# Emitting a triangular inverse one step at a time, with some of its VectorE instructions held in program order, and asking for one transfer of a recurrent chain before another

## The chip, the cores and the metric

The kernel runs on one core of one Trainium2 chip. A core has a matrix engine (TensorE, PE in the profile, with its weight loads as PEld), a vector engine (VectorE, DVE), a scalar engine (ScalarE, ACT), a general engine (GpSimd, POOL) and a sync engine (SyncE, SP). Each takes its own instructions in a fixed order and waits on semaphores for the others. Here SP issues the loads of weights, and POOL the transfers to and from scratch memory in HBM. The metric is the device time of one execution in microseconds (us), lower is better; the kernel before has a median of 1120.82 us in 3 runs (1118.6 to 1121.67).

## The reference, cut to what matters

One layer of a hybrid encoder over 512 tokens of 1024 channels. A normalised input is projected by one wide matrix; from the projections come a gated short convolution, a gated linear recurrence, and an RWKV-7 recurrence, which are merged by gates and projected; a squared-ReLU MLP and a last norm follow.

```python
h = rms_norm(x, norm1_g)
pa, pb, pg, pc = split(h @ w_in)                      # conv, linear recurrence, gates, RWKV-7
y_a = b_a * causal_dwconv(c_a * x_a)                  # "ab" in the kernel, with y_b
y_b = rg_lru(causal_dwconv(x_b)) * gelu(g_b)
def step(state, inp):                                 # RWKV-7, 16 heads of 64, over 512 tokens
    sa = einsum('bhvk,bhk->bhv', state, -kk_t)
    state = state * w_t + sa[..., None] * (kk_t * a_t) + v_t[..., None] * k_t
    y_t = einsum('bhvk,bhk->bhv', state, r_t)         # r is the receptance
m = gate_a * y_a + gate_b * y_b + gate_c * y_c
x = x + m @ w_out
x = rms_norm(x + square(relu(rms_norm(x) @ w1)) @ w2)
```

## The kernel before, in words

All large matrix products are done in three passes on split numbers: a weight tile `raw` (128x1024) is loaded by SP, ScalarE casts it to a rounded high part `whi` (L147, `ac.copy` in `split_w`), VectorE subtracts that from `raw` to give the low part `wlo` (the subtraction in `split_w`, shown as L104 because all `tensor_tensor` operations go through the helper `tt` there), and TensorE multiplies high by high (L168), high by low input (L169) and low by high (L170), 24 matmuls of 128x512 for a projection. There are two buffers of `raw` and three each of `whi` and `wlo`, so weights are ready at most about three projections ahead.

The RWKV-7 recurrence is done by chunks of 64 tokens. The 16 heads are four groups. For group g, `krv` computes keys, receptances and values (its row norm goes through a matmul `pn`, L433 and L434, on the halves `bh` and `bl` of squared keys, and back through VectorE: `rqw`, L194); `amat` computes the 64x64 matrices of each chunk; `inverse` inverts the triangular ones for 32 chunks and heads at once. In `inverse`, two transposes (L551) bring two 32x32 diagonal blocks each onto partitions; 31 steps of forward substitution follow on VectorE, each a multiplication into `dg` and an addition into `Z` (shapes 64x31 to 64x16x16 and down to 64x31), each of which depends on the one before; then three transposes (L568 twice, L571) bring the result back; then 32 small matmuls `pG` (L578) and 32 small `pT` (L588) make the off-diagonal block, and a POOL transfer stores the result in `ttd` (L591). I call the four calls inverse 0 to inverse 3.

The work of other parts is put between by `weave(crit, fill, r, base)`: it takes a step of the critical generator, adds `r` to a counter, and takes one step of the filler for each whole unit. A step of the critical generator is emitted under a raised priority (`base`, or the number that the generator yielded); the recorder then orders the instructions of each engine by priority and readiness by its own estimate of costs, so that the order in which they stand in the built program is fixed before it runs. The filler for inverse 0 to 2 is `fill_group`: 22 steps of the gate and recurrence branches `ab`, then `krv` of the next group with more of `ab` between, then 4 more; for inverse 3 it is `ab` alone. `keep_in_program_order` holds an instruction at its place in the program among those of its engine; before the change it is used for TensorE's small matmuls (by `pin`).

After the inverses, `chain` runs the 8 chunks one after another, with the rest of `ab` and then `gate` as filler. For each chunk `load_chunk` issues five transfers on POOL's queue, one chunk ahead: `sv` (values), `ax`, `tc` (the inverse), `bk` (keys) and, from chunk 1, `rt` (receptances). `bk` is used by the matmul `pS` (L664), `rt` by the matmul `py` (L645). After the chain come the output projection and the MLP, which the change does not touch.

Of the kernel before, what the change touches and what calls it, by code (L numbers as in the profile page):

```python
# [18 lines left out]
P = 128  # L19

OFF, OFFS, OFFP = 160, 20, 30
CP, CPI, CPK, CPC, CPN = 150, 0, 0, 20, 5
HOT = 6000

NINV, NG_T, N_LOAD = 19, 4, 6


N_KRV = 22
F_INV, F_KRV, F_GAP = 22, 16, 4
W3 = 3  # L30
R0, R1, R2, R3, R4 = 0.85, 1.15, 1.1, 1.7, 1.0
NWARM = 2
POOL_KT = (1, 3, 5, 6, 7)
S = 512
# [4 lines left out]
NG = 4  # L39
# [59 lines left out]
def block_kernel(ctx, tc, xt, win, par, mulr, sw, wout, w1, w2, fg, cst, eyes, out):  # L99
    nc = tc.nc  # L100
    v, ac, gp, pe, sy = nc.vector, nc.scalar, nc.gpsimd, nc.tensor, nc.sync

    def tt(o, a, b, op):
        return v.tensor_tensor(out=o, in0=a, in1=b, op=op)  # L104
# [7 lines left out]
    MUL, ADD, SUB, MAX = ALU.mult, ALU.add, ALU.subtract, ALU.max  # L112
# [431 lines left out]
    def inverse(g, G_):  # L544
        AXt = G_.AX
        Z = p1.tile([P, 2, 32, 32], F32, tag="Z", name="Z")
        la, xt = Z[64:128, 0], Z[64:128, 1]
        dg = p1.tile([P, 32, 32], F32, tag="dg", name="dg")
        tmp = dg[64:128].rearrange("p a b -> p (a b)")
        for b in range(2):  # L550
            v.transpose(la[32 * b:32 * b + 32].rearrange("l s t -> l t s"),  # L551
                        AXt[32 * b:32 * b + 32, 0, :, :, 32 * b:32 * b + 32].rearrange("s c e t -> s t (c e)"))
        gp.dma_start(xt.rearrange("l s t -> l (s t)"), eyes)

        yield
        yield
        for s in range(31):
            n, c = 31 - s, s + 1
            tv = tmp[:, 0:n * c].rearrange("l (c t) -> l c t", c=c)
            tt(tv, la[:, s, s + 1:32].unsqueeze(1).to_broadcast([64, c, n]),  # L560
               xt[:, 0:c, s:s + 1].to_broadcast([64, c, n]), MUL)
            tt(xt[:, 0:c, s + 1:32], xt[:, 0:c, s + 1:32], tv, ADD)
            if s % 2 == 1:
                yield
        TT = Z[0:64].rearrange("p a b c -> p (a b c)").rearrange("p (l t) -> p l t", t=L)
        gp.memset(TT[32:64, :, 0:32], 0.0)
        for b in range(2):
            v.transpose(TT[32 * b:32 * b + 32, :, 32 * b:32 * b + 32].rearrange("s l t -> s t l"),  # L568
                        xt[32 * b:32 * b + 32].rearrange("l s t -> l t s"))
        d1 = gs = dg  # L570
        v.transpose(d1[0:32], TT[0:32, :, 0:32])  # L571
        for _ in range(NINV):
            yield CPI
        for half in range(2):
            pg = pm.tile([P, 16, 32], F32, tag="pm", name="pG")
            for i in range(16):
                l = 16 * half + i
                pin(i, lambda: pe.matmul(pg[32:64, i], AXt[0:32, 0, l // 4, l % 4, 32:64], d1[0:32, l],  # L578
                                             start=True, stop=True))
            ac.copy(gs[32:64, 16 * half:16 * half + 16], pg[32:64])  # L580
            yield
        for _ in range(NG_T):
            yield 0
        for half in range(2):
            pg = pm.tile([P, 16, 32], F32, tag="pm", name="pT")
            for i in range(16):
                l = 16 * half + i
                pin(i + half, lambda: pe.matmul(pg[0:32, i], gs[32:64, l], TT[32:64, l, 32:64], start=True, stop=True))  # L588
            ac.copy(TT[0:32, 16 * half:16 * half + 16, 32:64], pg[0:32])
            yield  # L590
        gp.dma_start(ttd[:, :, g].rearrange("c t e x -> t c (e x)"),  # L591
                     TT.rearrange("t (c e) x -> t c (e x)", c=NC))
# [6 lines left out]
    def load_chunk(c):  # L599
        ax = C["ph2"].tile([P, NG, 2, 4, L], F32, tag="ax", name="ax", bufs=2)  # L600
        sv = C["ph2"].tile([P, NG, 4, L], F32, tag="sv", name="sv", bufs=2)
        tc_ = C["ph2"].tile([L, NG, 4, L], F32, tag="tc", name="tc", bufs=2)
        rt = C["ph2"].tile([P, 8, L], F32, tag="rt", name="rt", bufs=2)
        bk = C["ph2"].tile([P, 8, P], F32, tag="bk", name="bk", bufs=2)
        flat = lambda t: t.rearrange("p g a e t -> p (g a e t)") if len(t.shape) == 5 else \
            t.rearrange("p g e t -> p (g e t)") if len(t.shape) == 4 else t.rearrange("p x t -> p (x t)")
        gp.dma_start(flat(sv[64:128]), flat(vtd[c]))
        gp.dma_start(flat(ax), flat(axd[c]))
        gp.dma_start(flat(tc_), flat(ttd[c]))
        if c < NC - 1:  # L610
            gp.dma_start(flat(bk), flat(bkd[c]))
        if c > 0:
            gp.dma_start(flat(rt), flat(rtd[c]))
        return ax, sv, tc_, rt, bk

    def by_tile(t):
# [234 lines left out]
    for g in range(NG):  # L851
        if g:
            fgr = fill_group(g)
            weave(inverse(g - 1, GS[g - 1]), fgr, R1)
            drain(fgr)
        weave(amat(g, GS[g]), fl, 1.0)
    weave(inverse(NG - 1, GS[NG - 1]), fl, R2)
    pk_ctx.close()
    p1_ctx.close()
    ph2_ctx = ExitStack()  # L860
# [261 lines left out]
```

## Time and profile before

| what | value |
|---|---|
| median of 3 runs | 1120.82 us (1118.6 to 1121.67) |
| the profiled execution, its own time | 1119.94 us |
| its span in the trace | 1118.2 us |
| TensorE busy, matmuls | 1055.3 us, 94% of the span |
| VectorE busy | 746.4 us, 67% |
| ScalarE busy | 473.4 us, 42% |
| mean granted TensorE clock | 0.974 of full |

The 1.7 us between the profiled execution's time and its span lie around the span. The page shows the span in 40 slices of 28 us; the digits are busy tenths. Idle time of TensorE is named in the view of waits by what ended it; "us in total, times, longest us" follow the colon. In a timeline row come start, duration, engine, line, operation, output and inputs, shapes, count, and in square brackets the idle time of that engine before it and what ended it. A row of the windows view gives, for one stretch, its length, the busy time of each engine with its instructions, the granted TensorE clock and the share of the DMA engines.

### The profile page before, as it was taken

To read this page: it belongs to the slowest core of one execution; us is meant where nothing else is said; L and a number is where in the kernel's file an instruction comes from. 1 tells how busy PE (TensorE), PEld (TensorE's weight loads), DVE (VectorE), ACT (ScalarE), POOL (GpSimd) and SP (SyncE) were. 2 spreads that over 40 slices of the span, in tenths; PEclk is the share of its full clock that TensorE was granted. 3 is DMA by queue.
4 is the path that set the end of the run, shared out by engine and by line. 5 is a ranking of instruction groups with operands and counts; after the bars stand their busy time and mean duration, and the time that the engine had idled before them with its cause. 6 is when DMAs were issued, how large, how long until landed. Compare 5 with 4: busy or idle time off the path is not lost.

```text
span 1118.2 us, 16117 instructions
## 1 busy us (share of the span) xinstructions
PE 1055.3 (94%) x6396; PEld 863.6 (77%) x6396; DVE 746.4 (67%) x1276; ACT 473.4 (42%) x698; POOL 108.0 (10%) x167
## 2 busy tenths in 40 slices
PE   8899979999699979999898999899999999999997
PEld 5677857887587857887686888798888888888885
DVE  7997989789888998769846677965444443222224
ACT  6655345444364434534554444334344333112214
POOL 3212000210011001210021220101000000000001
PEclk8999989999899989999999999999999999999999
DMA  6243623562253523552278763234323335333321
GB/s 206 83 127 103 167 81 102 146 179 88 71 141 108 167 79 91 149 148 85 78 226 257 247 222 129 95 115 165 98 94 95 94 95 190 102 102 95 94 95 75
DMA packets 43323, 142.13 MB, mean 127 GB/s; under 512 B 5680, under 2 KB 9264, under 8 KB 42224
## 3 DMA queue, kind: packets, MB, share of 16 engines
q1 hardware_dynamic: 29472, 91.02, 25.7%
q0 software_dynamic: 13056, 49.03, 15.4%
q8 instruction: 50, 0.82, 0.3%
q10 hardware_dynamic: 720, 1.05, 0.3%
q14 instruction: 25, 0.20, 0.1%
HBM read 115.91 MB, written 25.17 MB: 126 GB/s over the span
## 4 chain that ended last, share of the span: by engine, by line
PE 61%; DVE 27%; issue 5%; DMA 4%; ACT 3%; POOL 1%; SPq 0%; DVEq 0%; POOLq 0%; ACTq 0%
PE pp L168 7%; PE pp L170 6%; PE pp L169 6%; PE acc L170 6%; PE acc L168 6%; PE acc L169 6%; PE p L168 5%; PE p L170 5%; PE p L169 5%; DVE wlo L104 5%; DVE Z L104 3%; DVE dg L104 3%; DVE g L107 2%; DMA rt<-rtd 2%; DVE u L107 2%
## 5 line engine op out<-in xcount | busy, mean ns | idle before, releaser
L104 DVE TENSOR_TENSOR wlo<-raw,whi 128x1024 fp32r<-128x1024 f32 (+1 forms) x164 | 199.6, 1218 | 249.6 <-ACT whi L147 247.9
L147 ACT CAST whi<-raw 128x1024 fp32r<-128x1024 f32 (+1 forms) x164 | 169.6, 1035 | 318.6 <-PE acc L170 126.3
L170 PE MATMUL pp<-hh,wlo 128*128 128x512 f32 x696 | 278.1, 400 | 21.6 <-DVE wlo L104 21.5
L168 PE MATMUL pp<-hh,whi 128*128 128x512 f32 x696 | 278.6, 401 | 4.1 <-ACT g L804 1.5
L169 PE MATMUL pp<-hl,whi 128*128 128x512 f32 x696 | 276.6, 397 | 2.8 <-DVE hl L107 2.8
L170 PEld LDWEIGHTS pp<-hh,wlo 128*128 128x128 f32 x696 | 133.6, 192 | 52.1 <-DVE wlo L104 24.2
L168 PEld LDWEIGHTS pp<-hh,whi 128*128 128x128 f32 x696 | 133.5, 192 | 35.3 <-ACT g L804 2.4
L169 PEld LDWEIGHTS pp<-hl,whi 128*128 128x128 f32 x696 | 133.4, 192 | 31.0 <-DVE hl L107 3.2
L170 PE MATMUL p<-h2h,wlo 128*128 128x512 f32 (+1 forms) x264 | 101.3, 384 | 0.0
L168 PE MATMUL p<-h2h,whi 128*128 128x512 f32 (+1 forms) x264 | 101.3, 384 | 0.0
L169 PE MATMUL p<-h2l,whi 128*128 128x512 f32 (+1 forms) x264 | 101.1, 383 | 0.0
L168 PE MATMUL acc<-whi,ah 128*128 128x512 f32 x256 | 99.6, 389 | 0.0
L169 PE MATMUL acc<-wlo,ah 128*128 128x512 f32 x256 | 99.6, 389 | 0.0
L170 PE MATMUL acc<-whi,al 128*128 128x512 f32 x256 | 99.6, 389 | 0.0
L170 PEld LDWEIGHTS p<-h2h,wlo 128*128 128x128 f32 x264 | 49.6, 188 | 9.7
L169 PEld LDWEIGHTS p<-h2l,whi 128*128 128x128 f32 x264 | 49.6, 188 | 9.6
L168 PEld LDWEIGHTS p<-h2h,whi 128*128 128x128 f32 x264 | 49.7, 188 | 9.5
L169 PEld LDWEIGHTS acc<-wlo,ah 128*128 128x128 f32 x256 | 48.0, 188 | 10.1
L170 PEld LDWEIGHTS acc<-whi,al 128*128 128x128 f32 x256 | 48.0, 188 | 10.0
L168 PEld LDWEIGHTS acc<-whi,ah 128*128 128x128 f32 x256 | 48.0, 188 | 9.9
L104 DVE TENSOR_TENSOR dg<-Z 64x31 f32<-64x31 f32 (+15 forms) x124 | 42.2, 340 | 4.1
L104 DVE TENSOR_TENSOR Z<-Z,dg 64x31 f32<-64x31 f32 (+15 forms) x124 | 42.2, 340 | 4.1
(296 smaller groups left out, 1455.0 us busy)
## 6 DMA issues: line engine op xcount, KB each, us to landing
raw<-in_win SPq DMA_DIRECT2D x88, 512.0 KB, 3.6
raw<-in_w SPq DMA_DIRECT2D x64, 512.0 KB, 3.5
ax<-axd POOLq DMA_DIRECT2D x8, 1024.0 KB, 7.5
axd<-AXt POOLq DMA_DIRECT2D x12, 512.0 KB, 7.2
bkd<-BKT POOLq DMA_DIRECT2D x4, 1024.0 KB, 13.8
raw<-in_wout SPq DMA_DIRECT2D x8, 512.0 KB, 3.9
bk<-bkd POOLq DMA_DIRECT2D x7, 512.0 KB, 5.6
swr<-in_sw SPq DMA_DIRECT2D x16, 128.0 KB, 2.6
```

The lines of the kernel that those rows point to most:

```text
L104: return v.tensor_tensor(out=o, in0=a, in1=b, op=op)
L107: return v.scalar_tensor_tensor(out=o, in0=a, scalar=s, in1=b, op0=op0, op1=op1)
L147: ac.copy(hi[:, sl], raw[:, sl])
L168: pe.matmul(ps, wh, xh, start=start, stop=False)
L169: pe.matmul(ps, wh, xl, start=False, stop=False)
L170: pe.matmul(ps, wl, xh, start=False, stop=stop)
```

## The change

In `inverse` the generator yields after each of the 31 substitution steps (before: after every second). The multiplication of every sixth step (s = 5, 11, 17, 23, 29) and the three closing transposes are held in program order. Two filler turns (`N_TT`) are put before each of the closing transposes and after the second, and the number of turns before `pG` goes from 19 to 7. The raised priority of the substitution steps goes from 150 to 20 (`CPV`), and the filler steps per turn from 1.15 to 0.87 (inverse 0 to 2) and from 1.1 to 0.9 (inverse 3). In `load_chunk` `rt` is issued before `bk`. No arithmetic is added or removed.

```diff
-CP, CPI, CPK, CPC, CPN = 150, 0, 0, 20, 5
+CP, CPV, CPI, CPC, CPN = 150, 20, 0, 20, 5
...
-NINV, NG_T, N_LOAD = 19, 4, 6
+N_TT, NINV, NG_T, N_LOAD = 2, 7, 4, 6
...
-R0, R1, R2, R3, R4 = 0.85, 1.15, 1.1, 1.7, 1.0
+R0, R1, R2, R3, R4 = 0.85, 0.87, 0.9, 1.7, 1.0
...
         for s in range(31):
             n, c = 31 - s, s + 1
             tv = tmp[:, 0:n * c].rearrange("l (c t) -> l c t", c=c)
-            tt(tv, la[:, s, s + 1:32].unsqueeze(1).to_broadcast([64, c, n]),
-               xt[:, 0:c, s:s + 1].to_broadcast([64, c, n]), MUL)
+            mm = tt(tv, la[:, s, s + 1:32].unsqueeze(1).to_broadcast([64, c, n]),
+                    xt[:, 0:c, s:s + 1].to_broadcast([64, c, n]), MUL)
+            if s % 6 == 5:
+
+                tc.keep_in_program_order(mm)
             tt(xt[:, 0:c, s + 1:32], xt[:, 0:c, s + 1:32], tv, ADD)
-            if s % 2 == 1:
-                yield
+            yield
         TT = Z[0:64].rearrange("p a b c -> p (a b c)").rearrange("p (l t) -> p l t", t=L)
         gp.memset(TT[32:64, :, 0:32], 0.0)
         for b in range(2):
-            v.transpose(TT[32 * b:32 * b + 32, :, 32 * b:32 * b + 32].rearrange("s l t -> s t l"),
-                        xt[32 * b:32 * b + 32].rearrange("l s t -> l t s"))
+            for _ in range(N_TT):
+                yield CPI
+            tc.keep_in_program_order(
+                v.transpose(TT[32 * b:32 * b + 32, :, 32 * b:32 * b + 32].rearrange("s l t -> s t l"),
+                            xt[32 * b:32 * b + 32].rearrange("l s t -> l t s")))
+        for _ in range(N_TT):
+            yield CPI
         d1 = gs = dg
-        v.transpose(d1[0:32], TT[0:32, :, 0:32])
+        tc.keep_in_program_order(v.transpose(d1[0:32], TT[0:32, :, 0:32]))
         for _ in range(NINV):
             yield CPI
...
         gp.dma_start(flat(tc_), flat(ttd[c]))
+        if c > 0:
+            gp.dma_start(flat(rt), flat(rtd[c]))
         if c < NC - 1:
             gp.dma_start(flat(bk), flat(bkd[c]))
-        if c > 0:
-            gp.dma_start(flat(rt), flat(rtd[c]))
...
-            weave(inverse(g - 1, GS[g - 1]), fgr, R1)
+            weave(inverse(g - 1, GS[g - 1]), fgr, R1, CPV)
...
-    weave(inverse(NG - 1, GS[NG - 1]), fl, R2)
+    weave(inverse(NG - 1, GS[NG - 1]), fl, R2, CPV)
```

First place: VectorE at the end of inverse 0. `wlo` is the low part of a weight tile for the filler, `u` and `g` are filler operations of `ab`, `ks` is a key row of `krv`, `Z` and `dg` belong to the inverse. Before:

```order
L104 TENSOR_TENSOR Z<-Z,dg 64x29x3
L104 TENSOR_TENSOR dg<-Z 64x60
L104 TENSOR_TENSOR Z<-Z,dg 64x30x2
L104 TENSOR_TENSOR dg<-Z 64x31
L104 TENSOR_TENSOR Z<-Z,dg 64x31
L568 STREAM_TRANSPOSE Z<-Z 32x32x32 x2
L571 STREAM_TRANSPOSE dg<-Z 32x1024
L104 TENSOR_TENSOR wlo<-raw,whi 128x1024
L107 SCALAR_TENSOR_TENSOR u_1163<-u_1353,u_1163 128x512
L104 TENSOR_TENSOR swbl<-swr,swbh 128x256
L104 TENSOR_TENSOR wlo<-raw,whi 128x1024
L107 SCALAR_TENSOR_TENSOR ks<-pp,part,ks 128x511
```

And now, from the tile that corresponds to the first `wlo` above:

```order
L104 TENSOR_TENSOR dg<-Z 64x156
L104 TENSOR_TENSOR wlo<-raw,whi 128x1024
L104 TENSOR_TENSOR Z<-Z,dg 64x26x6
...
L104 TENSOR_TENSOR dg<-Z 64x31
L104 TENSOR_TENSOR wlo<-raw,whi 128x1024
L104 TENSOR_TENSOR Z<-Z,dg 64x31
L573 STREAM_TRANSPOSE Z<-Z 32x32x32
L104 TENSOR_TENSOR u_1353<-u_1353,g_1164 128x512
L107 SCALAR_TENSOR_TENSOR ks<-pp,part,ks 128x511
L573 STREAM_TRANSPOSE Z<-Z 32x32x32
L107 SCALAR_TENSOR_TENSOR g_1164<-u_1353,u_1207 128x512
L104 TENSOR_TENSOR bl<-a_1378,bh 128x512
L578 STREAM_TRANSPOSE dg<-Z 32x1024
```

The two weight tiles that stood behind all three transposes now stand ahead of them, the first of them with eleven substitution operations behind it too, and filler operations stand between the transposes.

Second place: VectorE early in inverse 1, from the addition of the fifth step. Before:

```order
L104 TENSOR_TENSOR Z<-Z,dg 64x5x27
L104 TENSOR_TENSOR wlo<-raw,whi 128x1024
L104 TENSOR_TENSOR dg<-Z 64x156
L107 SCALAR_TENSOR_TENSOR u_2002<-u_2002,g_1944 128x512
L104 TENSOR_TENSOR Z<-Z,dg 64x6x26
L104 TENSOR_TENSOR dg<-Z 64x175
```

And now, with some filler rows left out:

```order
L104 TENSOR_TENSOR Z<-Z,dg 64x5x27
L104 TENSOR_TENSOR wlo<-raw,whi 128x1024
L107 SCALAR_TENSOR_TENSOR u_2002<-u_2002,g_1944 128x512
L104 TENSOR_TENSOR wlo<-raw,whi 128x1024
L107 SCALAR_TENSOR_TENSOR u_1917<-u_2153,u_1917 128x512
...
L789 MEMSET u_2147 128x1
...
L104 TENSOR_TENSOR wlo<-raw,whi 128x1024
L107 SCALAR_TENSOR_TENSOR g_1944<-g_1944,u_2171 128x512
L104 TENSOR_TENSOR dg<-Z 64x156
```

The multiplication 64x156 (s = 5) now stands behind 16 filler operations, four weight tiles among them, where it stood behind one weight tile.

Third place: POOL's queue at the chain's first loads. Before, from the transfer that stores the last inverse:

```order
L591 DMA ttd<-Z 64x8x256
...
L609 DMA tc<-ttd 64x1024
L611 DMA bk<-bkd 128x1024
L607 DMA sv<-vtd 64x1024
L608 DMA ax<-axd 128x2048
L609 DMA tc<-ttd 64x1024
L611 DMA bk<-bkd 128x1024
L613 DMA rt<-rtd 128x512
```

And now:

```order
L598 DMA ttd<-Z 64x8x256
...
L616 DMA tc<-ttd 64x1024
L620 DMA bk<-bkd 128x1024
L614 DMA sv<-vtd 64x1024
L615 DMA ax<-axd 128x2048
L616 DMA tc<-ttd 64x1024
L618 DMA rt<-rtd 128x512
L620 DMA bk<-bkd 128x1024
```

The receptance of chunk 1 stands ahead of its keys; the nine issues are otherwise in the same order.

## The prediction

> **What bounds the kernel now.** I read the page first, then the waits of TensorE, then TensorE's timeline where those waits end, then VectorE and the clock in the stretches around them.
>
> ```profile
> PE 1055.3 (94%) x6396; PEld 863.6 (77%) x6396; DVE 746.4 (67%) x1276; ACT 473.4 (42%) x698; POOL 108.0 (10%) x167
> ```
>
> TensorE is busy for 94%, so only its waits, and a clock below full behind them, can be won. The view of TensorE's waits has three lines above 3 us (total, times, longest):
>
> ```profile
> PE pp L170 <- DVE wlo L104: 21.5, 4, 7.7
> PE pn L433 <- ACT bh L163: 10.2, 4, 8.8
> PE py L645 <- DMA rt<-rtd: 4.2, 1, 4.2
> ```
>
> In TensorE's timeline they have these places (in brackets the idle time):
>
> ```profile
> 158.67 0.80 PE L170 MATMUL pp<-hh,wlo 128*128 128x512 f32 x1 [7.66 <-DVE wlo L104]
> ...
> 290.93 0.80 PE L433 MATMUL pn<-bh,bd 128*128 128x512 f32 x1 [8.76 <-ACT bh L163]
> ...
> 413.43 0.79 PE L170 MATMUL pp<-hh,wlo 128*128 128x512 f32 x1 [6.67 <-DVE wlo L104]
> ...
> 512.08 0.50 PE L170 MATMUL pp<-hh,wlo 128*128 128x512 f32 x1 [2.40 <-DVE wlo L104]
> ...
> 547.38 0.79 PE L170 MATMUL pp<-hh,wlo 128*128 128x512 f32 x1 [4.78 <-DVE wlo L104]
> ...
> 597.82 1.66 PE L645 MATMUL py<-St,rt 64*64 64x64 f32 x32 [4.16 <-DMA rt<-rtd]
> ```
>
> The first five lie at the ends of inverses 0 to 3 (two in inverse 3): 7.66 + 8.76 + 6.67 + 2.40 + 4.78 = 30.3 us; the sixth is the chain's. The windows view shows the granted clock just behind three of them (stretch, its length, busy us and instructions of PE, PEld, DVE, ACT, POOL, then PEclk):
>
> ```profile
> 158.00:164.00 6.00, 5.33 (x13) 4.17 (x14) 5.24 (x8) 4.09 (x7) 0.00 (x0) 0.50 0.57 194
> 413.00:421.00 8.00, 6.75 (x16) 4.83 (x17) 6.17 (x13) 1.34 (x2) 0.00 (x0) 0.52 0.44 131
> 512.00:516.00 4.00, 3.92 (x11) 3.10 (x12) 3.78 (x8) 0.26 (x1) 0.00 (x0) 0.61 0.48 135
> ```
>
> Busy time by one minus clock gives 5.33 x 0.50 = 2.7, 6.75 x 0.48 = 3.2 and 3.92 x 0.39 = 1.5 us more. A wait of only 2.40 us was followed by the 0.61.
>
> So TensorE sets the end. But what does it wait for in the stages of the inverses? The windows from each inverse's start to the weight tile at which TensorE last nearly catches VectorE say it (inverse 0, 1, 2, and 3 to its last wait):
>
> ```profile
> 113.90:207.70 93.80, 86.04 (x470) 69.87 (x469) 84.70 (x165) 44.35 (x63) 7.70 (x12) 0.95 0.42 120
> 241.50:308.80 67.30, 57.19 (x267) 45.73 (x266) 61.31 (x114) 29.24 (x42) 2.96 (x5) 0.92 0.36 106
> 366.80:461.10 94.30, 85.71 (x466) 68.79 (x465) 84.56 (x158) 42.49 (x61) 8.08 (x12) 0.95 0.39 118
> 503.60:547.40 43.80, 36.62 (x154) 29.41 (x152) 41.43 (x75) 16.96 (x23) 0.57 (x1) 0.96 0.26 78
> ```
>
> VectorE is busy for 84.7 of 93.8, 61.3 of 67.3, 84.6 of 94.3 and 41.4 of 43.8 us: it is a second bound, hidden by the 67% of the page. This decides my forecast, because the change takes nothing off VectorE. Of its 9.1 us left in the first stretch, over a third (164 gaps of some 0.03 us, 3.9 us) lies between instructions that follow each other without a wait; likewise 3.3, 3.8 and all 2.4 in the others. Real waits are 5.2, 2.7, 5.9 and 0 us. The largest, from VectorE's waits in the first three stretches:
>
> ```profile
> DVE rqw L194 <- PE pn L434: 2.1, 1, 2.1
> DVE g L107 <- ACT u L776: 0.7, 1, 0.7
> ...
> DVE bl L104 <- ACT bh L163: 1.4, 1, 1.4
> DVE wlo L104 <- ACT whi L147: 1.3, 2, 1.0
> ...
> DVE rqw L194 <- PE pn L434: 3.3, 2, 1.7
> ```
>
> **The change part by part.** *The stall itself, at inverse 0.* VectorE's rows:
>
> ```profile
> 148.88 0.32 DVE L104 TENSOR_TENSOR dg<-Z 64x156 f32<-64x156 f32 x1
> ...
> 152.41 3.83 DVE L568 STREAM_TRANSPOSE Z<-Z 32x1024 f32<-32x1024 f32 x2
> 156.27 1.23 DVE L571 STREAM_TRANSPOSE dg<-Z 32x1024 f32<-32x1024 f32 x1
> 157.44 1.17 DVE L104 TENSOR_TENSOR wlo<-raw,whi 128x1024 fp32r<-128x1024 f32 x1
> ```
>
> The `wlo` that TensorE waits for stands behind three transposes, 3.83 + 1.23 = 5.06 us. In the new order these, and eleven substitution instructions (all that follow the 64x156 of 148.88 until the transposes at 152.41: 2.8 us busy), stand behind it: it comes 7.9 us earlier. TensorE ran dry at 158.67 - 7.66 = 151.01, and the tile would be ready near 157.44 + 1.17 - 7.9 = 150.7: that wait is gone or under 1 us. But the 7.9 us are late elsewhere: `ks` stands now behind the first transpose and `bl` behind the second, both on the way to `pn`, so I expect a wait of 3 to 5 us at `pn`, and later ones at tiles. The account that counts is therefore VectorE's, up to the tile where the two engines meet again (pairs of rows for inverse 0, 1 and 2):
>
> ```profile
> 206.51 1.23 DVE L104 TENSOR_TENSOR wlo<-raw,whi 128x1024 fp32r<-128x1024 f32 x1
> 209.16 0.50 PE L168 MATMUL pp<-hh,whi 128*128 128x512 f32 x1 [0.25 <-ACT g L804]
> ...
> 307.61 1.21 DVE L104 TENSOR_TENSOR wlo<-raw,whi 128x1024 fp32r<-128x1024 f32 x1
> 309.95 0.39 PE L168 MATMUL pp<-hh,whi 128*128 128x512 f32 x1
> ...
> 459.92 1.23 DVE L104 TENSOR_TENSOR wlo<-raw,whi 128x1024 fp32r<-128x1024 f32 x1
> 463.77 0.39 PE L168 MATMUL pp<-hh,whi 128*128 128x512 f32 x1
> ```
>
> The first is done at 207.74 and TensorE begins with it at 209.16: 1.4 us of room; the second at 308.82 and 309.95: 1.1. By the order, two operations of 128x512 (0.7 us each by the `bl` row below) moved behind this tile, 1.4; other work covers the `rqw` and `g` waits, 2.8; one pinned multiplication (64x240 behind a `ul` that waits for ScalarE's `uh`) gives back about 1.0. That is 3.2, I take **3.0**, with ends 0 (pins eat it) and 4.6 (no pin wait, with part of the room).
>
> *Inverse 1.* Six operations, 4.45 us, moved behind the tile, and the 1.4 of `bl` goes. Against it stands the pin of s = 5, now behind 16 filler operations, several of which need ScalarE's chain and a tile that TensorE must free first:
>
> ```profile
> 242.51 1.05 ACT L147 CAST whi<-raw 128x1024 fp32r<-128x1024 f32 x1 [3.80 <-PE pp L169]
> ...
> 246.09 0.83 ACT L771 ACTIVATE u<-u,dv 128x512 f32<-128x512 f32 x1
> ```
>
> Before, VectorE filled this time with free substitution steps. With nothing but filler ahead of the pin it reaches the second `wlo` at about 242.2 and waits 1.4 for this cast to end at 243.56, then at about 244.8 waits 2.1 for L771 to end at 246.92, then 0.85 and 0.6 for the two activations behind: some 4.7 us. 4.45 + 1.4 - 4.7 = 1.2; I take **1.0**, with ends -4 (the walk lacks waits at the later pins) and 5.9 (no wait at the pin).
>
> [...]
>
> *Inverse 2.* By the order 0.75 moves behind the tile at 459.92, `rqw` waits of 1.7 go: 2.4, and its room is 463.77 - 461.15 = 2.6, so up to 5.0. I take **3.5**, ends 0 and 5.0.
>
> *Inverse 3.* VectorE has no wait here to cover, and its filler has no other group's `krv`. Two transposes and some steps stand now ahead of the tile after the next, and `pG` waits for the third transpose. **1.0**, ends 0 and 3.8.
>
> *The chain's transfer.* From the chain of waits, POOL's timeline, the view of the tile `bk`, and TensorE's timeline:
>
> ```profile
> 579.38 18.30 DMA rt<-rtd
> ```
>
> ```profile
> 578.84 0.58 POOL L611 DMA_DIRECT2D bk<-bkd  x1
> 579.38 0.58 POOL L613 DMA_DIRECT2D rt<-rtd  x1
> ```
>
> ```profile
> DMA to landing us min/median/max: 3.5/5.6/17.9
> ```
>
> ```profile
> 606.05 1.15 PE L664 MATMUL pS<-sv,bk 128*64 128x64 f32 x32
> ```
>
> `bk` (512 KB) is issued 0.54 us before `rt` (256 KB) and, as the slowest of its transfers (17.9), lands 1 us before it; `rt` at 597.7, needed when TensorE ran dry at 597.82 - 4.16 = 593.66. With `rt` first I estimate its landing 0.54 earlier by the issue, and some 2 us earlier by the bytes that no longer stand ahead of it (the two took turns, so not the whole 512 KB): about 595.1, a wait of 1.4. The gain is **2.8**, ends 0.5 (only the issue moves) and 4.4 (all, with some clock). `bk` then lands at about 597.7; its first use here is 606.05, so 8 us cover it.
>
> *More yields, lower filler rates and priorities* issue nothing new; they act only through the order, counted above.
>
> The sum: 3.0 + 1.0 + 3.5 + 1.0 + 2.8 = 11.3 us, 1119.94 - 11.3 = 1108.6. The profiled execution lies 0.9 below the median 1120.82, within the spread of the runs; I forecast **1109**.
>
> [...]
>
> **The rivals.** *B: the interleaving does what it could at best.* All real waits of VectorE in the four stretches (13.8) go, the room at the tight tiles (1.4 + 1.1 + 2.6) is used, operations moved add some 4 and `rt` gives 4: about 27, so 1093. For it: three quarters of the stall stand plainly behind transposes. Against: VectorE would have to be free of waits for 250 us while tied to ScalarE and TensorE by `rqw`, `u` and `whi`. If TensorE lost no time at all, it would be 30.3 + 7.4 + 4.2 + 1.7 = 44 less, 1076; VectorE's work forbids that.
>
> *C: only `rt` is left.* The pins' waits eat the 8.5 us of the inverses: 1119.94 - 2.8 = 1117, and within 0.3% (some 3.4 us, about what runs of this kernel can tell from no change) it is counted as the same.
>
> *D: the pins hold VectorE.* There are 20 pinned multiplications, five per inverse. Before, a step could go ahead while a filler operation waited; now, a pinned step and every step behind it stand behind each filler operation emitted ahead. The waits that VectorE shows for ScalarE and TensorE are 0.7 to 2.1 us each; at 1.3, 20 pins cost 26 us, of which I counted about 6. That gives 1108.6 + 20 = 1128.6. It decides from about 1.1 us a pin (22 in all) on. Against it: many pins find their filler ready, since the cast and copy of a tile come long before its `wlo`; for it: the walk of inverse 1, where the very first pin costs 4.7.
>
> That the change does not do what it says is excluded by the order for the first tile; for the wait of TensorE as a whole it is case C.
>
> **How the numbers follow.** The forecast (1104 to 1113) has a chance of 0.52; B 0.16 (from 1086 to 1104); C 0.20 (1113 to 1124, of which about 0.06 is still faster by over 0.3%); D 0.12, of which 0.11 slower by over 0.3%. Faster: 0.52 + 0.16 + 0.06 = 0.74; slower 0.11; same 0.15. The sum of the lower ends is 0 - 4 + 0 + 0 + 0.5, near 1123, that of the upper ends 4.6 + 5.9 + 5.0 + 3.8 + 4.4 = 24, 1096; they will not all fall on one side. For 8 of 10 I reach into B and C: **1097 to 1120**.
>
> **What would show it.** Right: in TensorE's waits, `pp` for `wlo` falls from 21.5 to below 10, in more and shorter pieces; `pn` keeps 4 us or more; `py` for `rt` is under 2. In VectorE's timeline the transposes stand apart, the wait of `rqw` is smaller, and new waits of 1 to 2 us stand early in inverse 1 ahead of the pinned 64x156. VectorE's share in the four stretches rises towards 0.95. Wrong: if each stretch is some 7 us shorter (B), then VectorE was not the bound that I take it for; if long waits stand ahead of pinned multiplications in all four inverses (D), the pins cost what I put at 6 us; if `rt` still ends TensorE's wait with 4 us, its landing is set by the transfers of the queue and not by its place.

## The result, and the profile after

The changed kernel takes 1109.52 us (median of 4 runs, 1107.98 to 1111.41) against 1119.87 us before (4 runs, 1118.6 to 1121.67). The ratio is 0.9907, with a 95% interval of 0.9883 to 0.9932: about 10 us, or 0.9%, faster. Forecast were 1109 and a range of 1097 to 1120. The profiled execution took 1108.38 us, its span is 1106.6 us.

The busy times of the page of after, and the main waits of its TensorE:

```profile
PE 1056.1 (95%) x6396; PEld 865.3 (78%) x6396; DVE 743.6 (67%) x1276; ACT 473.9 (43%) x698; POOL 108.9 (10%) x167
```

```profile
PE pn L433 <- ACT bh L163: 9.4, 4, 5.3
PE pp L170 <- DVE wlo L104: 7.6, 4, 5.8
PE pp L168 <- DVE ks L107: 4.6, 1, 4.6
...
PE pga L169 <- DVE ul L104: 1.8, 1, 1.8
PE py L652 <- DMA rt<-rtd: 1.5, 1, 1.5
```

Busy times are what they were; the wait for `wlo` fell from 21.5 to 7.6 us, that for `rt` from 4.2 to 1.5, while `pn` keeps 9.4 and a new wait of 4.6 for `ks` has come. TensorE's timeline shows where:

```profile
151.75 0.50 PE L170 MATMUL pp<-hh,wlo 128*128 128x512 f32 x1 [0.50 <-DVE wlo L104]
...
162.15 0.80 PE L433 MATMUL pn<-bh,bd 128*128 128x512 f32 x1 [5.34 <-ACT bh L163]
...
279.40 0.79 PE L433 MATMUL pn<-bh,bd 128*128 128x512 f32 x1 [3.35 <-ACT bh L163]
...
304.82 0.80 PE L170 MATMUL pp<-hh,wlo 128*128 128x512 f32 x1 [5.82 <-DVE wlo L104]
...
408.31 0.80 PE L168 MATMUL pp<-hh,whi 128*128 128x512 f32 x1 [4.59 <-DVE ks L107]
```

At inverse 0 the wait for the tile went from 7.66 to 0.50, and 5.34 came back at `pn`. At inverse 1 one wait of 8.76 became two, 3.35 and 5.82. At inverse 2 the 6.67 became 4.59.

To see what each stage gained, I cut the trace of each kernel at marks of TensorE that all kernels have: the first matmul `pB` of a group (it closes `amat`, ahead of inverse 0, 1, 2, 3; stages 0 to 3 begin there), and the first matmul of the first and the second `pS` of the chain. For before and after these cuts are the windows

```profile
107.27:232.12 124.85, 116.84 (x659) 95.19 (x659) 107.34 (x192) 56.23 (x81) 13.44 (x21) 0.96 0.43 124
232.12:358.99 126.87, 116.14 (x660) 93.73 (x659) 109.55 (x195) 59.80 (x87) 12.71 (x20) 0.96 0.42 117
358.99:484.99 126.00, 117.16 (x658) 94.74 (x658) 106.01 (x188) 56.03 (x80) 13.25 (x20) 0.96 0.41 118
484.99:589.83 104.84, 97.66 (x580) 79.35 (x580) 79.63 (x130) 53.28 (x78) 10.21 (x17) 0.97 0.50 144
589.83:606.05 16.22, 12.06 (x181) 9.77 (x180) 8.15 (x12) 6.10 (x9) 2.65 (x5) 0.89 0.85 250
```

```profile
107.49:229.34 121.85, 116.00 (x659) 94.63 (x659) 107.51 (x192) 56.60 (x81) 13.47 (x21) 0.97 0.45 127
229.34:357.69 128.35, 118.89 (x659) 96.86 (x658) 108.37 (x195) 59.52 (x87) 12.92 (x20) 0.95 0.41 115
357.69:480.04 122.35, 117.04 (x658) 95.50 (x659) 104.89 (x188) 56.09 (x80) 13.37 (x20) 0.96 0.44 121
480.04:582.65 102.61, 97.00 (x581) 78.07 (x581) 78.93 (x130) 53.57 (x78) 10.23 (x17) 0.98 0.50 148
582.65:594.75 12.10, 10.56 (x182) 8.56 (x181) 8.15 (x12) 6.11 (x9) 3.21 (x6) 1.00 1.02 288
```

so the stages are 3.0, -1.5, 3.65, 2.2 and 4.1 us shorter. Stage 1 became longer. The length of a row less its PE busy time is TensorE's idle time, and this fell in every stage: by 2.2, 1.3, 3.5, 1.6 and 2.6 us, 11.2 in all. The busy time, for the same matmuls, changed by -0.8, +2.8, -0.1, -0.7 and -1.5 us; the one stage in which it grew, stage 1, is the one in which PEclk fell (0.96 to 0.95). A cut of one execution has scatter of its own, so the table gives every run's stages; two pairs have one and the same order in the first four stages on TensorE, VectorE and ScalarE (before with "swap", after with "inverse").

| stage, us | 0 | 1 | 2 | 3 | first chunk | time, median |
|---|---|---|---|---|---|---|
| before | 124.85 | 126.87 | 126.00 | 104.84 | 16.22 | 1119.87 |
| after | 121.85 | 128.35 | 122.35 | 102.61 | 12.10 | 1109.52 |
| e1 swap only | 124.76 | 126.77 | 125.96 | 104.83 | 12.63 | 1115.74 |
| e2 inverse part only | 122.21 | 128.73 | 121.10 | 104.15 | 15.81 | 1113.15 |
| e3 after, no multiply-adds | 122.47 | 123.43 | 119.43 | 96.69 | 12.35 | 1096.93 |
| e4 before, no multiply-adds | 120.95 | 125.34 | 123.39 | 99.83 | 16.81 | 1108.16 |
| e5 first hold off | 122.32 | 123.63 | 124.11 | 102.66 | 11.47 | 1104.50 |
| e6 no holds on steps | 123.76 | 124.42 | 121.59 | 103.34 | 11.93 | 1108.39 |
| e7 priority 150 | 121.11 | 129.72 | 121.42 | 104.94 | 12.54 | 1109.74 |
| e8 added matmuls, tile | 121.07 | 132.43 | 121.27 | 102.68 | 11.58 | 1111.74 |
| e9 late transposes | 123.41 | 129.00 | 126.75 | 114.91 | 11.81 | 1126.51 |
| e10 added matmuls, pn | 121.54 | 130.48 | 121.04 | 105.34 | 15.18 | 1110.47 |
| e11 e5, receptance early | 121.02 | 124.47 | 121.12 | 103.92 | 10.98 | 1103.66 |
| e12 e11, products on GpSimd | 126.25 | 130.05 | 124.75 | 105.39 | 12.39 | 1117.32 |

e5 and e11 have one order too, and stage 2 is 124.11 and 121.12 there:

```profile
352.41:476.52 124.11, 118.01 (x659) 96.14 (x659) 105.44 (x188) 55.99 (x80) 13.22 (x20) 0.96 0.44 120
354.53:475.65 121.12, 115.28 (x658) 94.03 (x658) 104.61 (x188) 55.87 (x80) 13.23 (x20) 0.99 0.44 123
```

TensorE idles for 6.1 and 5.8 us of them; the rest of the difference is its clock, 0.96 and 0.99. So a single stage of a single execution is good to about 3 us, and idle time is the steadier measure of the two. Means over the two pairs give 2.8, -1.7, 4.3, 1.5 and 3.7 us, together 10.4.

### The profile page after: what moved, and what is told of

Read it like the earlier page. It is cut to its first block, busy times and chain, and to the rows that moved or that the text cites. A ratio compares the mean times of both kernels' runs of the same rounds, so it can differ in the third digit from the quotient of the medians.

```text
span 1106.6 us, 16112 instructions
## 1 busy us (share of the span) xinstructions
PE 1056.1 (95%) x6396; PEld 865.3 (78%) x6396; DVE 743.6 (67%) x1276; ACT 473.9 (43%) x698; POOL 108.9 (10%) x167
## 4 chain that ended last, share of the span: by engine, by line
PE 65%; DVE 21%; DMA 5%; issue 5%; ACT 3%; POOL 1%; SPq 0%; ACTq 0%; POOLq 0%; DVEq 0%
PE pp L168 8%; PE pp L169 7%; PE pp L170 7%; PE acc L170 6%; PE acc L168 6%; PE acc L169 6%; PE p L169 5%; PE p L168 5%; PE p L170 5%; DVE wlo L104 4%; DMA raw<-in_win 3%; DVE dg L104 2%; DVE Z L104 2%; DMA rt<-rtd 1%; DVE u L107 1%
```

## The experiments

Theory V (the prediction's): VectorE is a second bound in the stages of the inverses; what the change wins there is what VectorE gets to the tile earlier, and the transfer is a gain of its own. Rival S: VectorE is not the bound, the stalls come from the place of the transposes alone. Rival D: the held multiplications cost much.

**e1 and e2: the two parts apart.** The kernel before with only this, and the changed kernel without it:

```diff
+        if c > 0:
+            gp.dma_start(flat(rt), flat(rtd[c]))
         if c < NC - 1:
             gp.dma_start(flat(bk), flat(bkd[c]))
-        if c > 0:
-            gp.dma_start(flat(rt), flat(rtd[c]))
```

> Kernel before with only the receptance issued ahead of the keys; the order on TensorE, VectorE and ScalarE is that of the kernel before. If the parts add up as the two traces show them (TensorE's start of the second chunk's pS moved from 7.18 to 11.30 us ahead between the first and the second pS), the time falls by about 4.1 us, to 1115.8, and TensorE's wait for rt falls from 4.2 to about 1.5 us. If all of the gain of the change is in this transfer, 1109.5. If the keys turn into the new wait, no gain.

> Changed kernel with the transfers issued in the old order: only the inverse part of the change. If the parts add up: 7.4 us faster than before (3.0 - 1.5 + 3.7 + 2.2 by the stages of the two traces), about 1112.5, and the 4 us wait for rt is back. If all of the gain is in the transfer: 1119.9.

Measured: 1115.74 us for the swap (ratio to before 0.9952, 0.9938 to 0.9967) and 1113.15 for the rest (0.9931, 0.9914 to 0.9947). The product of the ratios is 0.9883, at the lower edge of the change's interval; the swap alone brought 4.7 us in these runs and the rest 7.3, together a little more than both in one kernel (10.4 in its own runs), but no more than the intervals allow. The parts add up. The gain is not the transfer alone. TensorE's waits in the two:

```profile
PE py L645 <- DMA rt<-rtd: 1.9, 1, 1.9
```

```profile
PE py L652 <- DMA rt<-rtd: 3.9, 1, 3.9
```

**e3 and e4: VectorE's work taken away.** In the changed kernel and in the kernel before:

```diff
-        for n in range(3):
+        for n in range(0):
             stt(u[:, 1 + n:], px[:, 0:S - 1 - n], pv(f"lc{2 - n}", q), u[:, 1 + n:], MUL, ADD)
...
-        stt(y[:, 1:], cs[:, 0:S - 1], pv("ca1", q), y[:, 1:], MUL, ADD)
-        stt(y[:, 2:], cs[:, 0:S - 2], pv("ca0", q), y[:, 2:], MUL, ADD)
```

> Changed kernel in which the filler's five shifted multiply-adds on VectorE (three of the convolution of the recurrence branch, two of the short convolution) are left out for every tile: some 0.75 us each, 18.7 us of VectorE's time inside the four inverse stages. None of TensorE's work is left out, and the inverse is whole. If VectorE is the second bound there, the time falls by 10 to 18 us, to 1092 to 1100 (TensorE has some 26 us of waits and half clock left there). If the stalls come only from the order around the inverse, it falls by less than 4 us: 1106 to 1110.

> Kernel before with the same five multiply-adds left out for every tile. If VectorE is the second bound, 10 to 18 us faster than before (1102 to 1110) with the transposes still standing together ahead of the weight tile. If the standing transposes alone set the stalls, less than 4 us faster (1116 to 1120).

Measured: 1096.93 and 1108.16 us, 12.6 below the changed kernel and 12.3 below before's 1120.48 in the same runs. Both lie in V's range and far from S's, in the kernel before too, where the transposes still stand together. TensorE did all its work. In the windows of the four stages VectorE has 35 instructions and 23.5 us less in e3 (24.0 in e4), more than the 18.7 us expected, so each us taken away was worth about 0.5 us. It is not one for one: in stage 0 of the changed kernel nothing was gained (122.0 in the mean, 122.47), in stages 1 and 3 about all of it. Of the 13 us by which the four stages are shorter, TensorE's idle time is 7.6 in e3 and 9.8 in e4; the rest is busy time, with the clock. Two things besides VectorE's load changed with the edit. Leaving instructions out lets the recorder order some 400 rows of VectorE anew, so a single stage here should not be read finely; and three of the five multiply-adds stand in the chain that leads to `uh` and `ul`, which TensorE multiplies, so that chain became shorter. TensorE's waits for it sum to only 1.8 us in after (`pga` for `ul`), so this cannot be the bulk of it directly.

**e5 and e6: the holds.** 

```diff
-            if s % 6 == 5:
+            if s % 6 == 5 and s > 5:
```

(e6: `if s > 99:`. Without the hold on the transposes the built order is row for row the same, so that one does nothing here. e5's edit takes the hold on s = 5 off in all four inverses, but the order changes in inverse 1 alone.)

> Changed kernel in which the multiplication of s = 5 is no longer held in program order (s = 11, 17, 23, 29 and the transposes still are). The built order differs from the changed kernel only in inverse 1. There VectorE waited 5.7 us ahead of that multiplication. By VectorE's account these waits go, but the six operations (4.45 us) that the hold had moved behind the tile stand ahead of it again: the stage gains 1 to 4 us, the more if the two waits of TensorE (3.35 and 5.82 us, each with half clock behind it) become one: 1105.5 to 1108.5. If the held multiplication is the whole loss of the stage, 5 us or more: below 1104.5. If the early hold is what helps, slower than 1110.5.

> Changed kernel in which no multiplication of the substitution is held in program order (the built order is the same with and without the hold on the three transposes, so those stay). If the holds on the steps are what gives the gain of the inverse part, the time goes back towards that of the swap alone, 1114 to 1116. If they cost what the rival of held VectorE says, 5 us or more faster, below 1104.5. If they only choose between orders of like worth, within 3 us of the changed kernel's 1109.5.

Measured: e5 1104.50 us (ratio 0.9852, 0.9835 to 0.9868), 5.0 below the changed kernel: more than the 1 to 4 that V gave, and just at the point from which the hold was to be the whole loss of the stage. e6 1108.39 (0.9889, 0.9871 to 0.9907), not to be told from the changed kernel. So the holds as a whole are not what gives the gain, and one of them costs. The intervals of e5 and e6 do not overlap either: the 3.9 us between them say that the other holds, taken together, bring something in a kernel without the first. Where they bring it no stage shows, since the profiled execution of e6 (1105.59 us) is the fastest of its five.

What the first hold costs is not what I thought. In the changed kernel VectorE's waits ahead of the held multiplication are there, as walked:

```profile
240.86 1.23 DVE L104 TENSOR_TENSOR wlo<-raw,whi 128x1024 fp32r<-128x1024 f32 x1 [1.53 <-ACT whi L147]
...
245.41 0.69 DVE L104 TENSOR_TENSOR u<-u,g 128x512 f32<-128x512 f32 x1 [1.47 <-ACT u L781]
...
255.48 0.32 DVE L104 TENSOR_TENSOR dg<-Z 64x156 f32<-64x156 f32 x1
```

But the tile at which the engines meet comes no earlier without these waits. In after and in e5:

```profile
303.55 1.23 DVE L104 TENSOR_TENSOR wlo<-raw,whi 128x1024 fp32r<-128x1024 f32 x1
```

```profile
302.99 1.23 DVE L104 TENSOR_TENSOR wlo<-raw,whi 128x1024 fp32r<-128x1024 f32 x1 [0.81 <-ACT whi L147]
```

Counted from the start of the stage (229.34 and 228.78) it is done at 75.44 and at 75.44 us: the six operations that stand ahead of it again take up the waits saved. The 4.7 us of stage 1 lie behind the tile:

```profile
304.80:357.69 52.89, 52.58 (x367) 42.51 (x367) 42.47 (x73) 26.31 (x40) 6.94 (x11) 0.92 0.43 122
```

```profile
304.24:352.41 48.17, 47.62 (x310) 38.32 (x308) 38.27 (x66) 25.70 (x39) 6.92 (x11) 1.00 0.46 131
```

TensorE hardly idles in either, but in after its clock is 0.92. The two rows do not hold the same work (367 matmuls and 310): the 64 small `pG` stand behind the tile in after and ahead of it in e5. Over the whole stage the work is the same. There TensorE idles for 9.5 us in after and 8.8 in e5, and its busy time is 118.89 and 114.87 us (e5's row stands with e9 below): 4.0 of the 4.7 us are the same matmuls taking longer. The second trace of each order agrees: busy 119.30 us in e2 and 115.72 in e11, idle 9.4 and 8.8. In after TensorE had run ahead through `pn` after a first wait of 3.35, stood 5.82 for the tile, and then went at half rate for 8.8 us, with the 64 `pG` in that time (3.62 us, 2.21 in e5); in e5 it stood once, 8.21 us at `pn`, and met the tile at full clock (1.00 over the 48.17 us behind it). Two waits had two stretches at half clock behind them (0.53 over 3.6 us, 0.50 over 8.8), the one wait of e5 one (0.63 over 4 us).

**e7: the priority.** `CPV` from 20 back to 150.

> Changed kernel with the raised priority of the substitution steps put back from 20 to 150. Most of the order stays (VectorE: 68 of 1278 rows differ). If the gain comes from the steps between the filler's operations and the turns ahead of the transposes, it stays within 2 us of 1109.5; if the lower priority is what puts the weight tiles ahead of the inverse, the stalls come back: 1113 or more.

Measured: 1109.74 us (0.9899, 0.9881 to 0.9916), the same: the lower number is not what gives the gain.

**e8 and e10: keeping the clock up.** e8 added 20 matmuls at the tile of inverse 1 in the changed kernel, e10 28 matmuls ahead of `pn` in e5's kernel:

```diff
+            if g in (2,) and jj == 0:
+                for i in range(28):
+                    pe.matmul(pn, bd, hh[:, 0], start=i == 0, stop=i == 28 - 1)
             pe.matmul(pn, bd, sqh, start=True, stop=False)
```

> Changed kernel with 20 more matmuls of 128x512 (4.5 us at full clock) at the tile whose low part TensorE waits for at the end of inverse 1 (5.82 us): they repeat the product of the high part of the weights with the low part of the input, so the output of that projection is not the reference's. If the half clock behind the wait (8.7 us of matmuls at about half rate) comes from the idle time, the work that is added costs nothing and the clock stays full there: 2 to 4 us faster than the changed kernel, 1105.5 to 1107.5. If the clock has another cause, 0 to 4.5 us slower.

> The same kernel (1104.5) with 28 more matmuls of 128x512 (6.3 us at full clock) into pn just ahead of the pn on which TensorE waits 8.2 us in inverse 1; their result is overwritten, so nothing is left out or changed in the output, and VectorE's order is the same. If the half clock behind a wait comes from the idle time itself, the wait shrinks to about 2 us, the clock behind it stays full (in that run 0.63 over 4 us), and the stage of inverse 1 is 1.0 to 1.8 us shorter. If the clock has another cause, the stage is as long as it was or longer, and PEclk behind the wait stays near 0.6.

Measured: 1111.74 and 1110.47 us, slower than their bases. Neither filled the wait. In e8 the recorder put `pG` ahead of most of the added work, and TensorE stood 4.89 us for `dg` first. In e10 it put `pn` and the added work ahead of a projection that used to run before the wait:

```profile
270.96 6.66 PE L435 MATMUL pn<-hh,bd 128*128 128x512 f32 x28
283.89 0.80 PE L436 MATMUL pn<-bh,bd 128*128 128x512 f32 x1 [6.27 <-ACT bh L163]
```

Stage 1 grew by 6.0 to 6.9 us over e11 and e5, about the 6.3 us that were added. That idle time as such, and not something that goes with it, causes the half clock is therefore argued from e5, not shown by taking it away.

**e9: the transposes later.** In e5's kernel, the turns ahead of and between the transposes:

```diff
-            for _ in range(N_TT):
+            for _ in range((8, 0)[b]):
                 yield CPI
...
-        for _ in range(N_TT):
+        for _ in range(0):
             yield CPI
```

> The kernel of the run with the first hold off (1104.5), with eight turns ahead of the first closing transpose and none between the three: in the built order the three transposes stand behind ks, bl, rqw and rs of every stage, so nothing that leads to pn stands behind them any more. If the waits at pn and for ks (15.0 and 4.6 us in that run) come only from where the transposes stand, they go, and the time falls by 8 us or more: below 1097. If VectorE's whole work ahead of the tile at which TensorE catches up sets the stage, they come back at a later place and the time stays within 4 us of 1104.5.

Measured: 1126.51 us (1.0044 of before, 1.0027 to 1.006), 22 us slower than e5. Both expectations missed it on the slow side. TensorE's waits:

```profile
PE pn L433 <- ACT bh L163: 13.1, 5, 6.5
PE pG L585 <- DVE dg L578: 10.7, 2, 8.1
PE pp L168 <- DVE ks L107: 4.6, 1, 4.6
```

With nothing of the closing transposes ahead of `ks`, the waits at `pn` still sum to 13.1 us (15.0 in e5) and `ks` costs 4.6 as before: their place makes little of these waits. TensorE's idle time in stages 0 to 2 is 5.4, 8.5 and 6.9 us, for 5.7, 8.8 and 6.1 in e5, so there the idle time did what the second expectation said. What grew is the busy time for the same matmuls. In stage 1 of e9 and of e5:

```profile
230.94:359.94 129.00, 120.47 (x659) 97.72 (x658) 109.12 (x195) 59.77 (x87) 12.86 (x20) 0.93 0.41 115
```

```profile
228.78:352.41 123.63, 114.87 (x660) 93.64 (x659) 108.55 (x195) 59.80 (x87) 12.86 (x20) 0.97 0.43 120
```

The clock is 0.93 for 0.97, and the 5.6 us of busy time are all by which the stage is longer. Over the four stages 14.0 us are busy time and 7.3 idle time, 7.0 of these in stage 3, where `pG` stood 8.1 us for `dg` and the chain began later; that part I put down to the eight turns ahead of the first transpose. So neither expectation had the term that counts most here, the clock, and why its half-rate stretches are longer in e9 stays open.

**e11: the receptance earlier still.** In e5's kernel `rt` of chunk 1 is loaded with chunk 0, behind its `bk`:

```diff
-        if c > 0:
+        if c > 1:
             gp.dma_start(flat(rt), flat(rtd[c]))
         if c < NC - 1:
             gp.dma_start(flat(bk), flat(bkd[c]))
+        if c == 0:
+            gp.dma_start(flat(rt), flat(rtd[1]))
+            C["rt1"] = rt
+        if c == 1:
+            rt = C["rt1"]
```

> The same kernel (1104.5) with the receptance of chunk 1 issued with the loads of chunk 0, four transfers earlier than in the change; all else in the same order. If place in POOL's queue sets its landing, TensorE's wait at the first py for rt is gone; the gain is 0 to 1.5 us, since in that run only 0.9 us of it are left: 1103 to 1104.5. If the bytes in flight set it, the wait moves to ax or tc of chunk 1 and the time is 0 to 3 us longer.

Measured: 1103.66 us (0.985, 0.9836 to 0.9865), 0.8 below e5, not to be told apart. No wait for `rt` is left. e5 and e11 are the fastest kernels of this study, some 16 us below before.

**e12: work moved to GpSimd.** In e11's kernel, three products of a tile:

```diff
-        tt(cs, xs, cs, MUL)
+        gp.tensor_tensor(out=cs, in0=xs, in1=cs, op=MUL)
...
-        tt(y, bs, y, MUL)
+        gp.tensor_tensor(out=y, in0=bs, in1=y, op=MUL)
...
-        tt(g2, g2, gb, MUL)
+        gp.tensor_tensor(out=g2, in0=g2, in1=gb, op=MUL)
```

> The kernel with the first hold off and the receptance early (1103.7) in which three products of each filler tile (short convolution's input and output gate, the cubic term of the gelu; 0.69 us each on VectorE) run on GpSimd, which is busy for 10% of the time. The output is the reference's. If VectorE's work is what the stages of the inverses wait for, the time falls by 4 to 9 us, to 1095 to 1100 (some five tiles lie in the stages, 2.1 us each; leaving out the multiply-adds brought 0.7 us of each us taken away). If the order of the instructions alone decides, or GpSimd's longer time for such a product (1.3 us) makes others late, 1103 or more.

Measured: 1117.32 us (0.9971, 0.996 to 0.9982), 13.7 slower than e11. It looked like a clean way to use what e3 had shown, and fails; one thing that went against it stands in e12's timelines of GpSimd and VectorE, side by side:

```profile
252.45 1.51 POOL L787 TENSOR_TENSOR u<-u,g 128x512 f32<-128x512 f32 x1 [13.73 <-DVE Z L104]
258.00 1.64 POOL L803 TENSOR_TENSOR g<-g,g 128x512 f32<-128x512 f32 x1 [4.04 <-ACT g L802]
```

```profile
252.40 0.41 DVE L104 TENSOR_TENSOR dg<-Z 64x247 f32<-64x247 f32 x1
252.85 1.39 DVE L104 TENSOR_TENSOR Z<-Z,dg 64x247 f32<-64x247 f32 x1
...
258.40 1.78 DVE L107 SCALAR_TENSOR_TENSOR u<-u,u 128x512 f32<-128x512 f32 x1
```

The addition 64x247 takes 0.41 us in e11 and 1.39 here: it begins while GpSimd's product runs and ends 0.28 us after it. The `u` of 0.69 us takes 1.78 in the same way. VectorE's busy time over the four stages is 401.6 us against 399.5 in e11, although its share of the 24 products left it, and it waits more for results that now come from GpSimd. TensorE's idle time over these stages is 36.8 us against 25.8, its busy time 449.7 against 444.7. So e12 took nothing off VectorE and does not test V; how its 13.7 us divide between lengthened instructions, later results and the order that changed with them stays open.

## Why the prediction came out

**What held.** VectorE as the hidden second bound is the step that carried the forecast. TensorE's waits and half clock around the inverses and the chain came to 44 us; the order alone, read without VectorE, would have given most of them back, and the change brought 10. e3 and e4 show that the stages follow VectorE's time, in part, and e9 that freeing `ks` and `bl` from the transposes does not free `pn`. For inverse 1 VectorE's account came out nearly to the digit: a gain of 1.2 was walked, and the tile was done 76.70 us after the start of the stage before (308.82 - 232.12) and 75.44 after. The five terms are sums of waits, and as waits they all came out: 3.0, 1.0, 3.5, 1.0 and 2.8 us were forecast, and TensorE's idle time fell by 2.2, 1.3, 3.5, 1.6 and 2.6 (in e1 and e2, whose orders are those of before and after, the first four are 2.4, 1.2, 3.6 and 2.8). The stall reappeared at `pn` (3 to 5 us forecast, 5.34 came), the wait for the tile of inverse 0 fell under 1 us (0.50), and neither rival C nor D took place: e2 shows 7 us from the inverses alone, e6 that the five holds cost or bring nothing in sum.

The transfer's working held in both its parts. In the chain of waits of after:

```profile
571.68 16.24 DMA rt<-rtd
```

16.24 against 18.30 us from issue to landing, 2.06 of the "some 2 us" for the bytes, and 0.54 for the issue; 1.54 us of the wait are left, 1.4 were forecast. That `bk` and `rt` "took turns" was an estimate: in before they were in flight together from 579.38 us on and landed at 596.7 and 597.7, and how they shared the queue in that time no run shows.

**Where terms were off, and cancelled.** The sum of 11.3 has five terms; against the means over the pairs, which hold idle time and clock together:

- Inverse 0, 3.0 forecast, 2.8 measured, partly for another reason. VectorE's waits were to fall by 2.8 less 1.0; counted as gaps of 0.1 us or more, they went from 5.5 to 5.2 us, since new ones stand in for the old. (The prediction's 5.2 rests on 164 gaps of some 0.03 us, 3.9 in sum; there are 107, 3.5 in sum. Nothing hangs on it.) The tile came 1.7 us earlier (98.8 us into the stage for 100.5), most of it from the two operations moved; the rest is the room of 1.4 us, which TensorE has used up: it begins the tile within 0.1 us of its end.
- Inverse 1, +1.0 forecast, -1.7 measured: the one wrong sign. The failing step is that the account that counts was taken to be VectorE's alone: it fixes when TensorE gets the tile, not at which clock it goes on. I had rows of half clock behind three of the stalls and counted nothing for the clock, as if its loss stayed what it was. The idle time fell by 1.3 us as walked; the busy time grew by 2.8, which I put down, by e5, to the single wait that turned into two, each with half clock behind it (0.53 and 0.50).
- Inverse 2, 3.5 forecast, 4.3 measured; VectorE's tile came 3.5 us earlier (102.2 and 98.6 us into the stage), 2.4 of it walked, and the room went from 2.6 to 2.4.
- Inverse 3, 1.0 forecast, 1.5 measured, within the scatter of a stage.
- The transfer, 2.8 forecast, 3.7 measured (4.7 in e1's times). The missing part is the clock again: over the matmuls behind the wait it was 0.79 before and 1.00 after.

```profile
597.82:606.05 8.23, 8.23 (x82) 6.47 (x82) 1.66 (x3) 0.63 (x2) 0.53 (x1) 0.79 0.66 244
```

```profile
588.06:594.75 6.69, 6.69 (x83) 5.24 (x83) 4.03 (x6) 1.90 (x3) 1.09 (x2) 1.00 1.01 310
```

The 8.23 us at 0.79 are 1.7 us lost (the 1.7 that rival B's sum of 44 uses without a row); the shorter wait of 1.54 left the clock full. That is not assured by the shorter wait: in e10, with the same order of transfers, 2.00 us for `rt` were followed by 0.57 over 4 us, and the first chunk took 15.18.

So 1109 came out because 2.7 us lost in inverse 1 stand against 0.8, 0.5 and 0.9 that came better elsewhere. The bound by VectorE, and with it the idle time, is what was understood. The clock was put at nothing, and that its shifts nearly cancel over the five terms (-0.4 us of busy time in the two traces) is luck.

**What a wait costs in clock.** The prediction had the 0.61 behind a wait of 2.40 us and has no term for the clock in its sum. The length of a wait alone does not say, in these traces, which clock follows. In after, 3.35 us were followed by half clock, and 5.82 by half clock for almost 9 us:

```profile
279.40:283.00 3.60, 3.60 (x9) 2.87 (x10) 2.78 (x6) 1.53 (x2) 0.00 (x0) 0.53 0.09 34
304.80:313.60 8.80, 8.78 (x76) 7.20 (x77) 7.12 (x10) 2.42 (x4) 0.00 (x0) 0.50 0.38 119
```

But in the same trace 1.52 us cost the clock too (0.61 over the 4 us behind it), where the 1.54 for `rt` left it full (1.00):

```profile
691.56 0.62 PE L168 MATMUL acc<-mh,whi 128*128 128x256 f32 x3 [1.52 <-ACT mh L720]
```

```profile
691.56:695.56 4.00, 3.26 (x15) 3.06 (x16) 3.97 (x9) 1.02 (x3) 2.71 (x4) 0.61 0.61 210
```

And one and the same wait goes both ways. The first `pB` waits 1.58 us in before and 1.57 in e4; the 4 us behind it are

```profile
107.27:111.27 4.00, 4.00 (x26) 3.62 (x27) 3.95 (x4) 3.31 (x6) 2.42 (x4) 1.00 0.31 60
```

```profile
107.38:111.38 4.00, 4.00 (x19) 3.92 (x20) 3.95 (x4) 2.09 (x4) 2.09 (x3) 0.57 0.31 60
```

The granted clock that is kept with the traces of before and of after is either 1.00 or 0.50. In both, every stretch of half clock but the one at the very end lasts 3.41 us or two or three times as long, and within a trace all begin on one grid of 3.41 us. At inverse 0 the stretch is from 154.49 to 164.73 us in before and from 159.98 to 166.80 in after; counted from the start of the span the grid lies 2.07 us later in after. That what a wait costs depends also on where it falls on that grid is my estimate from these traces; no run moves a wait against it. Idle time is not all that counts. In after the step of the grid from 306.75 to 310.17 has no idle time and is mostly `pG`, and the clock stays at half behind it; the step from 436.46 to 439.87 has none either, is mostly `pT` and at full clock, and the next is at half. These are the only such steps in after, and before has none; that these small matmuls are the cause is not shown.

What was wrong was to count a split of a wait as neutral. In stage 1, where the wait is in two pieces (after, e2, e7), TensorE is busy for 118.9 to 121.1 us; where it is in one (before, e1, e5, e6, e11), for 114.9 to 116.1. That does not hold for e9, whose order differs more: 6.5 us in one wait, 0.6 in another, and 120.5 us busy. Waits in pieces that all left the clock full are seen here only in stage 3 of e3 and e4 (1.00 over the stage), where work of VectorE was left out.

## What to carry to other kernels

Where an engine is hidden behind the page's average, compute the windows of the stage before believing that a stall can be scheduled away: here the tile was reached 1.7, 1.3 and 3.5 us earlier in stages 0 to 2, and TensorE's idle time fell by 2.2, 1.3 and 3.5. Then price the clock behind each new piece of a split wait, because one long wait can be cheaper than two of middling length (8.21 us in e5 with 114.9 us busy in stage 1, 3.35 and 5.82 in after with 118.9), and give that price a range: here the same order of instructions gave stages up to 3 us apart. When two kernels are compared by stage, take idle and busy time of the bounding engine apart. A hold in program order behind filler that waits for another engine should be judged one by one; here taking the first of five off was worth half as much as the whole change.

## What was not expected of the hardware

A product of 128x512 on GpSimd took 1.3 to 2.4 us in e12, and most instructions of VectorE that began in its time took longer than the same ones in e11: 0.41 became 1.39 (`Z` of 64x247), 0.69 became 1.78 (`u` of 128x512), 0.27 (a `dg` of 64x112) became 1.34 us. These three end 0.28, 0.54 and 0.13 us after GpSimd's product. Of the 23 rows of VectorE's timeline that begin during one of the 24 moved products 16 are longer, and 7 are not, among them a `v` of 128x511 (0.74 us in both). What the two engines share no run shows. What can come of it in a kernel that VectorE bounds e12 shows: with the 24 products moved it was 13.7 us slower, later results and a new order included.
